# A streaming softmax: the exit of the engines with one barrier around the clearing of the semaphores instead of two

## The chip, the cores and the metric

One of the eight cores of a Trainium2 chip. The metric is the device time of one execution in microseconds; a profile of one execution comes with it. Most executions of this kernel agree within 0.3%. "Span" is the stretch from the first to the last profiled instruction; a store "lands" when its last semaphore update is in the trace.

## The reference

```python
x = np.random.randn(16, 1024, 512).astype(np.float32)
x_max = np.max(x, axis=-1, keepdims=True)
exp_x = np.exp(x - x_max)
return (exp_x / np.sum(exp_x, axis=-1, keepdims=True)).astype(np.float32)
```

A softmax over rows of 512 numbers: 33.55 MB in, 33.55 MB out.

## The kernel before

SyncE issues the loads, VectorE takes the row maxima and scales, ScalarE takes the exponentials and issues the stores. GpSimd and PE compute nothing in the body. The launch wraps the body in a context whose end adds an exit to every engine's program:

```python
with _tile.TileContext(nc) as tc:            # the launch line: L175 in the kernel before
    tile_softmax_online_kernel(tc, *args)
# ... cut: in the body, the last group's scaling ends with the last store
            nc.scalar.dma_start(
                out=dst[k][:, since:b, :], in_=place[k][:, since:b, :]
            )
```

This is the exit as it stands in the built program, engine by engine. "Gather" counts arrivals, "release" counts permissions to leave; `>=` and `== 0` are waits. A drain lets its engine's earlier work end first: VectorE's first one starts at 141.54 us and ends at 144.73, just after the last multiply.

```
SP    five semaphore waits and a drain: all loads, all stores, ScalarE, VectorE
ACT, PE, DVE, SP   drain, release == 0, gather += 1   (first arrival)
                   wait release >= 1, -= 1     (first leave)
                   drain, release == 0, gather += 1   (second arrival)
                   wait release >= 1, -= 1     (second leave)
POOL  drain
      wait gather >= 4, -= 4                   (first gather)
      release += 4                             (first release)
      drain
      clear the range of semaphores 99 to 108  (those of the body)
      drain
      wait gather >= 4, -= 4                   (second gather)
      release += 4                             (second release)
```

After it the runtime's own code runs; the profile does not show its instructions, but the trace has semaphore updates that come after the last profiled instruction, and I put these down to it.

Of the kernel before, what the change touches and what calls it, by code (L numbers as in the profile page):

```python
# [1 line left out]

# [4 lines left out]

F32 = mybir.dt.float32
EXP = mybir.ActivationFunctionType.Exp
AX = mybir.AxisListType.X  # L10


CHUNKS = [
    (3, 0), (5, 3), (8, 8), (16, 16), (16, 32), (16, 48), (16, 64), (16, 80), (16, 0), (16, 16),
]
SBUF_ROWS = 96

EARLY = 8
AFTER_STORE = {2: [8], 3: [9]}

GROUP = 8

FINISH_BEFORE = (1, 2, 3)

STORE_ROWS = {3: 8, 4: 8, 5: 8}

ON_ACT = ()

AT_HEAD = {mybir.EngineType.SP: 3}



def loads_at_the_head(nc):

    main, body = nc.main_func.blocks[0], nc.main_func.blocks[1]
    for engine, count in AT_HEAD.items():
        loads = [
            i
            for i in body.instructions
            if i.engine == engine and type(i).__name__ == "InstDMACopy"  # L40
        ][:count]
        barrier = next(
            n
            for n, i in enumerate(main.instructions)
            if i.engine == engine and type(i).__name__ == "InstDrain"
        )
        for load in loads:
            body.instructions.remove(load)
        main.instructions[barrier:barrier] = loads


@with_exitstack
def kernel(
    ctx: ExitStack,
    tc: tile.TileContext,
    x: bass.AP,
    out: bass.AP,
):
    nc = tc.nc
    nc.at_finalize(loads_at_the_head)  # L60
    P = nc.NUM_PARTITIONS

    x_flat = x.flatten_outer_dims()
    out_flat = out.flatten_outer_dims()
    n, d = x_flat.shape
    assert n == P * sum(R for R, _ in CHUNKS)


    src, dst, at = [], [], 0
    for R, _ in CHUNKS:  # L70
        for flat, views in ((x_flat, src), (out_flat, dst)):
            part = flat[at : at + P * R, :]
            views.append(part.rearrange("(p r) d -> p r d", r=R))
        at += P * R

    data = ctx.enter_context(tc.tile_pool(name="data", bufs=1))
    stats = ctx.enter_context(tc.tile_pool(name="stats", bufs=4))
    held = data.tile([P, SBUF_ROWS, d], F32, name="held")
    place = [held[:, s : s + R, :] for R, s in CHUNKS]


    groups = []
    for k, (R, _) in enumerate(CHUNKS):
        m = -(-R // GROUP)
        cuts = [R * i // m for i in range(m + 1)]
        since = 0
        for a, b in zip(cuts, cuts[1:]):
            ends = b == R or b - since >= STORE_ROWS.get(k, R)
            groups.append((k, a, b, since if ends else None))
            since = b if ends else since  # L90
    shift = [None] * len(groups)
    sums = [None] * len(groups)

    def load(k):
        queue = nc.scalar if k in ON_ACT else nc.sync
        queue.dma_start(out=place[k], in_=src[k])

    def rowmax(g):
        k, a, b, _ = groups[g]
        shift[g] = stats.tile([P, b - a], F32, name="shift", tag="shift")  # L100
        nc.vector.reduce_max(  # L101
            out=shift[g], in_=place[k][:, a:b, :], axis=AX, negate=True
        )

    def exps(g):
        k, a, b, _ = groups[g]
        sums[g] = stats.tile([P, b - a], F32, name="sums", tag="sums")
        for r in range(a, b):
            nc.scalar.activation(  # L109
                out=place[k][:, r, :],  # L110
                in_=place[k][:, r, :],
                func=EXP,
                bias=shift[g][:, r - a : r - a + 1],
                scale=1.0,
                accum_out=sums[g][:, r - a : r - a + 1],
            )

    def scale(g):
        k, a, b, since = groups[g]
        recip = stats.tile([P, b - a], F32, name="recip", tag="recip")  # L120
        nc.vector.reciprocal(out=recip, in_=sums[g])  # L121
        for r in range(a, b):
            nc.vector.tensor_scalar_mul(  # L123
                out=place[k][:, r, :],
                in0=place[k][:, r, :],
                scalar1=recip[:, r - a : r - a + 1],
            )
        if since is not None:
            nc.scalar.dma_start(
                out=dst[k][:, since:b, :], in_=place[k][:, since:b, :]  # L130
            )
        if b == CHUNKS[k][0]:
            for later in AFTER_STORE.get(k, ()):
                load(later)

    with tc.manual_schedule():
        for k in range(EARLY):
            load(k)
        waiting = None
        for g, (k, a, _, _) in enumerate(groups):  # L140
            if waiting is not None and a == 0 and k in FINISH_BEFORE:
                scale(waiting)
                waiting = None
            rowmax(g)
            exps(g)
            if waiting is not None:
                scale(waiting)
            waiting = g
        scale(waiting)


# [1 line left out]
_INS = ['x']  # L153
_OUTS = [((16, 1024, 512), 'float32')]


# [23 lines left out]
```

## Time and profile before

| | before |
|---|---|
| median time, 6 runs | 161.59 us (161.46 to 161.76) |
| span of the profiled instructions | 159.678 us |
| last store landed | 158.803 us |
| from that landing to the end of the span | 875 ns |
| from the end of the span to the runtime's last semaphore update | 1,901 ns |

The last two rows are what the argument is about: the exit, in the fourth, is half a percent of the time. Its instructions are semaphore instructions and drains, which the profile does not count as busy, so the engine shares, the slices and the chain of waits are blind to it. One finds it only by asking for the instructions of the launch line in the last two microseconds and by looking at where each starts. The prediction shows those lines.

### The profile page before, as it was taken

Reading aid. Unit: us, or ns where it says so; the run is one execution under the profiler, and the core shown is the slowest. Engines: PE = TensorE matmul, PEld = TensorE weight load, DVE = VectorE, ACT = ScalarE, POOL = GpSimd, SP = SyncE. Lnnn points to the kernel's source line nnn. Section 1 sums busy time; section 2 is a strip of 40 time slices with the busy share of each in tenths; the row PEclk is TensorE's granted clock in tenths of the full one; section 3 lists DMA queues with packets and bytes.
Section 4 is the critical chain, followed back from the end, with each engine's and each line's share of the span. In section 5 each row is a group of like instructions: output and inputs, shape, how many; then the busy total and the mean of one; then the engine's idle time right before and its main releaser. Section 6 shows DMA issues by size and latency. Waiting matters only on the chain.

```text
span 159.7 us, 521 instructions
## 1 busy us (share of the span) xinstructions
DVE 123.9 (78%) x162; ACT 93.3 (58%) x257; POOL 0.2 (0%) x4
## 2 busy tenths in 40 slices
DVE  0481870799699999999999999999999999762000
ACT  0718029208994959595867777686859594930000
POOL 0000000000000000000000000000000000000000
DMA  7999999899999999999999999999999999999993
GB/s 274 436 464 424 389 425 464 375 404 466 410 445 443 456 415 412 439 415 480 419 415 427 410 501 410 412 435 402 447 439 476 402 419 484 402 419 460 427 410 164
DMA packets 3315, 67.13 MB, mean 420 GB/s; under 512 B 368, under 2 KB 368, under 8 KB 624
## 3 DMA queue, kind: packets, MB, share of 16 engines
q1 hardware_dynamic: 1440, 33.56, 49.5%
q10 hardware_dynamic: 1872, 33.56, 48.9%
q14 instruction: 3, 0.02, 0.0%
HBM read 33.55 MB, written 33.55 MB: 420 GB/s over the span
## 4 chain that ended last, share of the span: by engine, by line
DVE 71%; ACT 14%; issue 3%; DMA 3%; DVEq 0%; ACTq 0%
DVE shift L101 38%; DVE held L123 30%; ACT held L109 14%; DMA held<-in_x_dram 3%; DVE recip L121 2%; DVEq L175 0%; ACTq L109 0%
## 5 line engine op out<-in xcount | busy, mean ns | idle before, releaser
L109 ACT ACTIVATE held<-held,shift 128x512 f32<-128x512 f32 x128 | 90.5, 708 | 43.4 <-DVE shift L101 33.3
L101 DVE TENSOR_REDUCE shift<-held 128x8 f32<-128x4096 f32 (+2 forms) x17 | 70.7, 4163 | 4.4 <-DMA held<-in_x_dram 4.4
L123 DVE TENSOR_SCALAR held<-held,recip 128x512 f32<-128x512 f32 x128 | 52.2, 482 | 0.6
L109 ACT ACTIVATION_READ_ACCUMULATOR held<-held,shift 128x1 f32 x128 | 23.9, 186 | 0.0
L121 DVE RECIPROCAL recip<-sums 128x8 f32<-128x8 f32 (+2 forms) x17 | 3.3, 195 | 15.8 <-ACT held L109 15.8
L109 ACT ACT_TABLE_LOAD x1 | 1.3, 1283 | 4.4 <-DMA held<-in_x_dram 4.4
L164 POOL MEMSET const-bfloat16-1.0<- 128x1 bf16 x1 | 0.1, 102 | 0.0
L164 POOL MEMSET const-uint8-127<- 128x1 uint8 x1 | 0.1, 102 | 0.0
L164 POOL MEMSET const-float32-1.0<- 128x1 f32 x1 | 0.1, 99 | 0.0
L164 POOL MEMSET const-float32-0.0<- 128x1 f32 x1 | 0.1, 98 | 0.2 <-issue 0.2
## 6 DMA issues: line engine op xcount, KB each, us to landing
held<-in_x_dram SPq DMA_DIRECT2D x7, 4096.0 KB, 41.8
out_dram<-held ACTq DMA_DIRECT2D x4, 4096.0 KB, 21.0
out_dram<-held ACTq DMA_DIRECT2D x7, 2048.0 KB, 35.4
held<-in_x_dram SPq DMA_DIRECT2D x1, 2048.0 KB, 11.4
held<-in_x_dram SPq DMA_DIRECT2D x1, 1280.0 KB, 7.0
out_dram<-held ACTq DMA_DIRECT2D x1, 1280.0 KB, 20.0
held<-in_x_dram SPq DMA_DIRECT2D x1, 768.0 KB, 4.4
out_dram<-held ACTq DMA_DIRECT2D x1, 768.0 KB, 15.8
```

Source lines behind the costliest of these rows:

```text
L101: nc.vector.reduce_max(out=shift[g], in_=place[k][:, a:b, :], axis=AX, negate=True)
L109: nc.scalar.activation(out=place[k][:, r, :], in_=place[k][:, r, :], func=EXP, bias=shift[g][:, r - a : r - a + 1], scale=1.0, accum_out=s ...
L121: nc.vector.reciprocal(out=recip, in_=sums[g])
L123: nc.vector.tensor_scalar_mul(out=place[k][:, r, :], in0=place[k][:, r, :], scalar1=recip[:, r - a : r - a + 1],)
L164: nc = _bacc.Bacc("TRN2", target_bir_lowering=False, num_devices=1)
```

## The change

The intent is to take one of the two barriers off the end of the kernel: the clear needs all engines to have arrived before it, and nobody to leave before it is done, and one gather ahead of it and one release behind it give both. A hook edits the exit block once the program's instructions are laid down (cut to the lines that matter):

```diff
+def one_barrier_on_exit(nc):
+    end = nc.main_func.blocks[2].instructions
+    def of(engine, kind):
+        return [i for i in end if i.engine == engine and type(i).__name__ == kind]
+    for engine in (... Activation, PE, DVE, SP ...):          # cut
+        arrivals = [i for i in of(engine, "InstDrain") if i.has_update()]
+        leaves = of(engine, "InstEventSemaphore")
+        assert len(arrivals) == len(leaves) == 2
+        end.remove(leaves[0])
+        end.remove(arrivals[1])
+    gather, release, gather_2, release_2 = of(mybir.EngineType.Pool, "InstEventSemaphore")
+    end.remove(release)
+    end.remove(gather_2)
...
     nc.at_finalize(loads_at_the_head)
+    nc.at_finalize(one_barrier_on_exit)
```

GpSimd keeps gather, drain, clear, drain, release. Nothing else in the program moves.

More of the change, by code (lines that the diff above doesn't have):

```diff
@@ L49, in loads_at_the_head @@
         main.instructions[barrier:barrier] = loads
+def one_barrier_on_exit(nc):
+    end = nc.main_func.blocks[2].instructions
+    def of(engine, kind):
+        return [i for i in end if i.engine == engine and type(i).__name__ == kind]
+    for engine in (
+        mybir.EngineType.Activation,
+        mybir.EngineType.PE,
+        mybir.EngineType.DVE,
+        mybir.EngineType.SP,
+    ):
+        arrivals = [i for i in of(engine, "InstDrain") if i.has_update()]
[6 more added lines that the diff above has]
+    end.remove(gather_2)
 @with_exitstack
```

## The prediction

> **What bounds the kernel now.** I read the page first, then the stretches of the last microseconds, then the launch line's own instructions there, then what SyncE waits for. The page's lines on busy time, the forty slices and the chain that ended last:
>
> ```profile
> DVE 123.9 (78%) x162; ACT 93.3 (58%) x257; POOL 0.2 (0%) x4
> ...
> DMA  7999999899999999999999999999999999999993
> ...
> HBM read 33.55 MB, written 33.55 MB: 420 GB/s over the span
> ...
> DVE 71%; ACT 14%; issue 3%; DMA 3%; DVEq 0%; ACTq 0%
> ```
>
> The sixteen DMA engines are at nine tenths or more in nearly every slice, VectorE at 78%, ScalarE at 58%. So this is a kernel that streams 67 MB and is held by its transfers. The chain by line is dominated by VectorE, but it ends with the last multiply at 144.7 us: it follows compute instructions, and none runs later. From there to 159.7 us the last store drains, and after it comes what this change edits. The stretches of the end (columns: stretch and its length, then busy us of VectorE, ScalarE, GpSimd, then the clock, the DMA share and GB/s):
>
> ```profile
> 150.00:155.00 5.00, 0.00 (x0) 0.00 (x0) 0.00 (x0) 1.00 1.06 459
> 155.00:156.00 1.00, 0.00 (x0) 0.00 (x0) 0.00 (x0) 1.00 0.68 295
> 156.00:157.00 1.00, 0.00 (x0) 0.00 (x0) 0.00 (x0) 1.00 1.14 492
> 157.00:158.00 1.00, 0.00 (x0) 0.00 (x0) 0.00 (x0) 1.00 0.16 66
> 158.00:159.00 1.00, 0.00 (x0) 0.00 (x0) 0.00 (x0) 1.00 0.00 0
> 159.00:160.00 1.00, 0.00 (x0) 0.00 (x0) 0.00 (x0) 1.00 0.00 0
> ```
>
> Data moves until about 158 us, and the last 1.7 us moves nothing. The last store was issued at 144.71 us and its semaphore is complete at 158.80 us. The waits of SyncE between 157 and 160 us (waiter, what it waited for, us in total, times, longest):
>
> ```profile
> SPq L175 <- DMA out_dram<-held: 9.6, 1, 9.6
> SPq L175 <- PEq L175: 0.6, 2, 0.4
> ```
>
> SyncE stood 9.6 us on the stores, so it is the last engine to arrive at the exit. The second line is the two releases it then waited for; the profile names PE there, but both come from GpSimd. The exit itself, as the launch line's instructions from 158 us on (engine, operation, count: ns shortest/median/longest, first and last start):
>
> ```profile
> L175 SPq EVENT_SEMAPHORE  x4: 17/22/28, 158.8 to 159.6; - x4
> L175 POOLq EVENT_SEMAPHORE  x4: 17/17/17, 159.0 to 159.6; - x4
> L175 SPq DRAIN  x3: 7/7/7, 158.9 to 159.2; - x3
> L175 ACTq EVENT_SEMAPHORE  x2: 17/17/17, 159.2 to 159.6; - x2
> L175 DVEq EVENT_SEMAPHORE  x2: 21/21/21, 159.2 to 159.6; - x2
> L175 PEldq EVENT_SEMAPHORE  x2: 51/51/51, 159.2 to 159.6; - x2
> L175 POOLq DRAIN  x2: 34/52/70, 159.2 to 159.4; - x2
> ...
> L175 POOLq EVENT_SEMAPHORE_RANGE_CLEAR  x1: 93/93/93, 159.3 to 159.3; - x1
> ```
>
> All of the two barriers and the clearing is here, between 159.0 us and the end of the span at 159.678 us. GpSimd's starts, to the nanosecond from the trace's records, are: gather 159.037, release 159.115, drain 159.196, clear 159.295, drain 159.417, second gather 159.495, second release 159.574. The others pass the first release at 159.157 to 159.169 and the second at 159.615 to 159.627; PE's takes 51 ns and ends the span.
>
> **What the Trainium skill says.** "Perfetto Trace Analysis", section "Sequencer-only Instruction (DRAIN, etc)", says that only the execution of such an instruction is in the record, while waiting for a semaphore and spreading its update are not. The trace agrees: GpSimd's semaphore instructions record 17 ns each, yet the next instruction starts 78 to 81 ns after such a one starts. So I cost each instruction by the distance between starts, not by its duration. "VectorE: DVE Perf Modes", section "The DRAIN you can't avoid", puts boilerplate drains at about 12 ns on all engines. Here they take 7 to 19 ns on the four arriving engines, but 34 and 70 ns on GpSimd, the one that matters; the measurement decides. "Runtime: NRT & Kernel Launch", section "The ~15µs preamble/postamble breakdown", lists a barrier and semaphore reset that the runtime adds after the kernel. The time before is 161.66 us and the span 159.68 us, so about 2.0 us lies outside the profiled instructions; the change touches none of it.
>
> **The change part by part.** The body is untouched: the build shows the same sequence of loads, stores and compute on every engine. The end block falls from 30 instructions to 20.
>
> *Removed from ACT, PE, DVE and SP*: the first leave and the second arrival, two instructions each. These ran at 159.157 to 159.34 us, beside GpSimd's drain and clear. The second arrivals start at 159.249 to 159.319 us, and the latest is recorded as an update at 159.341 us, 154 ns before GpSimd's second gather starts at 159.495. They held nobody up, so removing them is worth 0 by itself.
>
> *Removed from GpSimd*: the first release and the second gather. GpSimd was on the path throughout: no other engine could leave before its second release, and it waited for nobody after 159.04 us. The first release costs the distance from its start to the drain's: 159.196 - 159.115 = 81 ns. The second gather costs the distance to the second release: 159.574 - 159.495 = 79 ns. Sum 160 ns.
>
> *Kept on the path*: gather, drain, clear, drain, one release, the leave. From the same SyncE arrival: gather at 159.037, drain 78 later at 159.115, clear 99 later at 159.214, drain 122 later at 159.336, release 78 later at 159.414, then 104 ns from that release to the end of PE's leave (159.574 to 159.678), ending at 159.518 us. That is 159.678 - 159.518 = 0.160 us less.
>
> *Added*: nothing. Nor does the clear come too early: it runs after all four have arrived, and SyncE arrives only after it has seen the last store's semaphore. The cleared numbers (98 to 108) do not include the barrier's own two (96 and 97), so a count in flight is not lost.
>
> Time: 161.66 - 0.16 = 161.50 us, or 0.1% less.
>
> **The rivals.** *A whole barrier is saved.* From GpSimd's drain at 159.196 us to the end is 482 ns, and a barrier without a clear might seem to cost most of that: 161.2 us. Against it: 99 + 122 ns of that stretch is the drain and the clear, which stay, and the exit after the release stays too. Even this would be 0.3%.
>
> *The clear moves into the wait and is hidden.* Were the clear done while SyncE still waits for stores, the path would lose another 0.2 us (161.3 us). Against it: the clear still stands after the gather in GpSimd's order, so it starts after the last arrival.
>
> *A new wait takes the removed one's place.* The four engines now sit at one release from their arrival on, and the runtime's own barrier follows. If that barrier, or the sequencers' fetching after a longer wait, absorbed the gain, the time would stay 161.66. For it: the profile shows nothing of the runtime's code but its length. Against it: before, too, all engines leave within 12 ns of one another on one release and enter that code together, so the shape should only shift. Instruction fetches were at 44.6, 61.0 and 101.5 us, none near the exit.
>
> *The gain drowns.* Three runs before spread over 0.24 us, more than the 0.16 expected, because the body's transfers vary. This rival concerns what is seen, not what happens, and I think it likely with three runs.
>
> **Range and chances.** Mechanism: 0.16 us, with 0.08 (one of the two instructions absorbed) to 0.3 as its outer bounds, so 161.36 to 161.58. The spread of the runs before, about 0.12 us either side, and a shift between sessions widen this to 161.20 to 161.78. For faster by 2% the kernel would have to lose 3.2 us; the entire stretch from SyncE's arrival to the end is 0.67 us. Within 2% is nearly certain; I leave 1% for each side, for a disturbed session.
>
> **What would show it.** GpSimd should have two semaphore instructions at the exit in place of four, still two drains and one clear, and the other engines one semaphore instruction and one arriving drain each. From SyncE's arrival to the end of the span should be near 0.51 us in place of 0.67. From GpSimd's gather to its drain should be near 78 ns and from its second drain to the release near 78 ns; if either is near 160, the removed instruction's time was a wait and not a step. If the exit shrinks but the difference between the time and the span grows, the runtime's barrier took the gain. The store's landing at 158.8 us should move only by run-to-run noise; if it moves by more than 0.3 us, the comparison of single profiles says nothing of the exit. The prediction would be wrong if the body changed, which the build denies, or if engines left the release apart.

## The result, and the profile after

The changed kernel took 161.41 us, median of 6 runs (161.38 to 161.66), against 161.59 us before (161.46 to 161.76). A ratio here is the mean time of one kernel's fast runs over that of the other's in the same rounds, so not quite the ratio of the medians. It is 0.9991, with a 95% interval from 0.9979 to 1.0004: the same within 2%, and by these runs alone not even surely below 1.

The page of the changed kernel, the lines that answer to those of before (busy time, slices, bytes, chain by engine), with the line of the span:

```profile
span 159.6 us, 511 instructions
...
DVE 123.9 (78%) x162; ACT 93.3 (58%) x257; POOL 0.2 (0%) x4
...
DMA  7999999899999999999899999999999999999993
...
HBM read 33.55 MB, written 33.55 MB: 421 GB/s over the span
...
DVE 71%; ACT 14%; issue 3%; DMA 3%; DVEq 0%; ACTq 0%
```

There are ten instructions fewer, and otherwise it is the same page: the body is untouched, and on this scale the exit is invisible. What SyncE waits for between 157 and 160 us, after the change:

```profile
SPq L199 <- DMA out_dram<-held: 9.6, 1, 9.6
SPq L199 <- PEq L199: 0.5, 1, 0.5
```

There is one wait for a release now, where before there were two (0.6 us in all). The launch line is L199 in the changed kernel; its instructions from 158 us on (engine, operation, count: ns shortest/median/longest, first and last start in us):

```profile
L199 SPq EVENT_SEMAPHORE  x3: 17/27/28, 158.9 to 159.5; - x3
L199 SPq DRAIN  x2: 7/7/7, 159.0 to 159.1; - x2
L199 POOLq EVENT_SEMAPHORE  x2: 17/17/17, 159.1 to 159.5; - x2
L199 POOLq DRAIN  x2: 34/52/70, 159.2 to 159.4; - x2
L199 POOLq EVENT_SEMAPHORE_RANGE_CLEAR  x1: 93/93/93, 159.3 to 159.3; - x1
...
L199 PEldq EVENT_SEMAPHORE  x1: 51/51/51, 159.5 to 159.5; - x1
```

GpSimd has two semaphore instructions where it had four, and PE one where it had two. The starts of GpSimd's instructions from the trace's records, in ns after its first gather, and the end of the span on the same scale:

```
          gather  release  drain  clear  drain  gather  release   end of span
before         0       78    159    258    380     458      537           641
changed        0        -     81    180    302       -      365           469
```

The exit is 172 ns shorter: 78 ns between the gather and the first drain (159 to 81) and 94 ns between the second drain and the release (157 to 63). The stretch ahead of the gather is 234 ns from the last landing in both kernels, so the landing to the end went from 875 to 703 ns. Yet the profiled execution's time fell by only 0.05 us, 161.46 to 161.41. Part of that is the body: its last store landed 80 ns later in this execution (158.883 us). The rest is outside the span: the time less the span is 1.782 us before and 1.824 us after.

So three questions were left. Is the saving the two GpSimd steps, or a hand-over between engines that went with them? Does the time follow the exit at all? And where do the 42 ns outside the span come from?

### The profile page after: what moved, and what is told of

It is laid out like the page before. It is cut to its first block, busy times and chain, and to the rows that moved or that the text cites. A ratio compares the mean times of both kernels' runs of the same rounds, so it can differ in the third digit from the quotient of the medians.

```text
span 159.6 us, 511 instructions
## 1 busy us (share of the span) xinstructions
DVE 123.9 (78%) x162; ACT 93.3 (58%) x257; POOL 0.2 (0%) x4
## 2 busy tenths in 40 slices
DMA packets 3315, 67.13 MB, mean 421 GB/s; under 512 B 368, under 2 KB 368, under 8 KB 624
## 4 chain that ended last, share of the span: by engine, by line
DVE 71%; ACT 14%; issue 3%; DMA 3%; DVEq 0%; ACTq 0%
DVE shift L125 39%; DVE held L147 30%; ACT held L133 14%; DMA held<-in_x_dram 3%; DVE recip L145 2%; DVEq L199 0%; ACTq L133 0%
```

## The experiments

Theory: each GpSimd instruction between the last arrival and the release is a step of about 80 ns on the path, whether it waits for anyone or not, and the change saves two steps. Rivals: the saving is the round trip to the other engines; or what follows the exit absorbs what the exit saves. Lengths below are of one execution's trace, "landing" is the last store's. All kernels gave correct results. `like(i, ...)` makes a copy of an exit instruction with other waits or updates, `sync(i, ...)` puts such a copy in its place.

### The changed kernel again, five rounds

> The changed kernel again, with more rounds. My theory (two steps of GpSimd left the path, and the runtime's part after the exit is unchanged): from the last store's landing to the end of the span 0.70 us where the kernel before has 0.875, and a time 0.16 to 0.18 us below the kernel before, ratio 0.9989 to 0.9990. Rival (what follows the exit absorbs the gain): ratio 1.000 with an exit of 0.70 us all the same.

Landing to end: 703 ns. Median 161.44 us (161.40 to 161.48) against 161.66 us, ratio 0.9985, interval 0.9972 to 0.9997: just below 1. The means differ by 0.24 us (161.68 and 161.44), more than the exit gives; the nine runs before spread from 161.55 to 161.93 us. So the sign is confirmed, if barely, but the time alone cannot tell 0.13 us from 0.17 us here; the larger edits below test that better. The time less the span averages 1.84 us in these five runs and 1.78 us in the nine before (each rounded to 0.1 us in the span), and this kernel's own trace has 1.837 us, so the 42 ns of the two profiles was no accident.

### One half: only the first release gone

```diff
-    end.remove(leaves[0]); end.remove(arrivals[1])
-    end.remove(release); end.remove(gather_2)
+    end.remove(leaves[0])
+    end.remove(release)
+    # each engine arrives twice in a row; the first gather waits for all eight
+    sync(gather, wait=[changed(w, wait_value=8) for w in gather.sync_info.on_wait])
```

> One half of the change: GpSimd's first release and the four first leaves are gone, the second barrier's arrivals and gather stay, and the first gather waits for both arrivals of each engine (8) so that the clear stays safe. My theory: from GpSimd's first gather to the end of the span 641 - 81 = 560 ns, since one GpSimd step is gone; the second arrival of SyncE adds some 58 ns ahead of the gather, so the landing to the end is about 0.85 us. Rival (the saving is in the second gather, which waits for arrivals): 641 ns from the first gather to the end, the gather being on the path as before.

Gather to end: 563 ns; the first drain starts 81 ns after the gather, and the second gather stays 78 ns behind the second drain. SyncE's second arrival cost 77 ns where 58 were expected (311 ns from the landing to the gather), so the landing to the end is 874 ns and not 850: this half gained a GpSimd step and gave a SyncE step back. Theory right, rival (641 ns) out. It shows why halves of such an edit need care: an instruction that was hidden before lay on the path here.

### The other half: the second gather gone, a step in the release's place

```diff
     end.remove(leaves[0]); end.remove(arrivals[1])       # as in the change
-    end.remove(release)
+    # the release becomes an addition to a body semaphore that nobody waits for any more
+    sync(release, update=[changed(u, id=99, update_value=1) for u in release.sync_info.on_update])
     end.remove(gather_2)
```

> The other half: second arrivals, second gather and first leaves are gone, but in the place of the first release GpSimd keeps one semaphore instruction that adds 1 to a semaphore that nobody waits for by then (it is cleared next). My theory (what counts is the number of GpSimd steps, about 80 ns each, whether or not anyone is released): 469 + 80 = 549 ns from the gather to the end of the span, against 641 before and 469 after the change. Rival (the cost is the hand-over to the four engines and their return): 469 ns, as with the whole change.

Gather to end: 547 ns, 78 more than the changed kernel and 94 less than before. So the two halves, 78 for the first release (above) and 94 for the second gather, add up to the 172 of the whole. An instruction that releases nobody costs as much as the first release did. The hand-over to the other engines was worth nothing: the 78 ns are GpSimd's step.

### The step by itself, ten times

```diff
+    # on top of the last edit: ten of the idle additions in a row, between the gather and the drain
+    end[at:at] = [like(step) for _ in range(9)]
```

> The disputed cost by itself, ten times: the changed kernel with ten such idle semaphore instructions on GpSimd between the gather and the drain. My theory: 10 x 80 = 0.80 us more than the changed kernel from the gather to the end (1.27 us), and the time too rises by 0.80 us over the changed kernel, 0.63 us over the kernel before (ratio 1.0039), since what follows the exit absorbs nothing. Rival one (the runtime's part absorbs exit time): the span grows but the time stays. Rival two (an instruction that releases nobody costs only its recorded 17 ns): 0.17 us more.

The launch line's instructions in this kernel, from 159.1 us on, the GpSimd lines:

```profile
L233 POOLq EVENT_SEMAPHORE  x12: 17/17/17, 159.4 to 160.5; - x12
...
L233 POOLq DRAIN  x2: 34/52/70, 160.2 to 160.4; - x2
L233 POOLq EVENT_SEMAPHORE_RANGE_CLEAR  x1: 93/93/93, 160.3 to 160.3; - x1
```

Twelve instructions of 17 ns fill more than a microsecond: the records of their starts lie 78 or 79 ns apart, and the gather to the end is 1,253 ns, 784 more than in the changed kernel. The time rose with it: the mean is 162.27 us, 0.83 us above the changed kernel in the same session (161.44). Ratio to the kernel before 1.0033 (1.0017 to 1.0048). So what follows the exit absorbs nothing of this size, and a recorded duration of 17 ns is not the cost.

### Ten more whole barriers

```diff
+    for n in range(10):        # after the exit: every engine arrives and leaves, GpSimd gathers and releases
+        for engine in four:
+            more += [like(arrival), like(leave)]
+        more += [like(gather), like(release)]
```

> The changed kernel with ten more whole barriers (arrive, gather, release, leave) after its exit. My theory: a bare barrier costs its round trip, worked out from the trace of the kernel before: gather to release 78 ns, release to PE's leave 54, leave to PE's next arrival 150, arrival to gather 33, together 315 ns; so 3.15 us more span and time than the changed kernel (time ratio to the kernel before 1.018). It is more than the 0.17 us that the change saved, because the removed barrier's round trip lay beside the drain and the clear. Rival (a barrier costs what the change saved): 1.7 us more. Rival two (the 482 ns from the drain to the end are a barrier's price): 4.8 us more.

The launch line's instructions from 158.9 us on:

```profile
L235 POOLq EVENT_SEMAPHORE  x22: 17/17/17, 159.1 to 162.8; - x22
...
L235 PEldq EVENT_SEMAPHORE  x11: 51/51/51, 159.5 to 162.8; - x11
...
L235 PEldq DRAIN  x10: 7/8/8, 159.7 to 162.7; - x10
```

Ten barriers took 3,315 ns, 331 each on average: gather to release 78, release to the next gather 249 in the common case, so 327. PE arrives last each time; once, where its arrival came some 80 ns after VectorE's and not 40, the barrier took 366. The exit is 3,142 ns longer than before the change, and the mean time 3.11 us longer (164.70 and 161.59 us; ratio 1.0192, 1.0178 to 1.0206, an interval that holds the 2% mark). Both rivals are out: a bare barrier costs neither the 172 ns that the change saved nor 482. The theory's sum of 315 ns was 5% short: PE's arrival to the gather takes 44 ns in the first of them, and the 33 of the sum were SyncE's. The change saved half a barrier because the other half, the second arrivals, had run beside the drain and the clear.

### Without the drains around the clear

```diff
+    for drain in of(mybir.EngineType.Pool, "InstDrain")[1:]:
+        end.remove(drain)
```

> The changed kernel without GpSimd's two drains around the clear. My theory (each remaining GpSimd instruction is a step on the path): gather to clear about 80 ns, clear to release 93 + 30 = 123 ns, release to the end 104 ns, so 307 ns from the gather to the end against 469; about 0.16 us saved. Rival (the drains cover a time in which the clear or its spreading must finish anyway): the release moves little, and more than 400 ns remain.

Gather to end: 308 ns. The clear starts 81 ns after the gather and the release 122 ns after the clear, as if the drains had never stood between. Another 161 ns gone, and the rival (the drains cover a time that must pass anyway) is out. That they may be dropped safely is less than shown: the result was right, and GpSimd has nothing in flight at this point; its last compute instructions are the four memsets at the start.

### GpSimd waits for the last store itself

In the changed kernel SyncE sees the last landing, then passes one more wait, a drain and its arrival, and only then does GpSimd start: 234 ns after the landing.

```diff
+    store = [w for w in waits if w.id == 107]      # the last store's semaphore
+    rest = [w for w in waits if w.id != 107]
+    sync(last, wait=rest)                          # SyncE no longer waits for it
+    sync(gather, wait=list(gather.sync_info.on_wait) + store)
```

> The changed kernel, with the wait for the last store moved from SyncE to GpSimd's gather: SyncE arrives early, and GpSimd goes on straight from the landing. My theory: SyncE's three steps and its arrival (234 ns from the landing to the gather's start) fall to about 20 ns; the landing to the end is 0.02 + 0.47 = 0.49 us against 0.70, and the time 0.21 us below the changed kernel, 0.38 below the kernel before (ratio 0.9976). Rival (a wait for two semaphores on GpSimd is slower, or wakes late): no gain, 0.65 us or more.

Landing to end: 482 ns (0.49 us expected). The mean time is 161.22 us against 161.59, ratio 0.9977 (0.9961 to 0.9992).

### Both shortenings together

> Both shortenings together on the changed kernel: GpSimd waits for the last store itself, and the two drains around the clear are gone. My theory: 0.02 + 0.31 = 0.33 us from the landing to the end, against 0.875 before: 0.55 us off the time, ratio 0.9966, clear of 1. Rival (what follows the exit has its own floor): the exit shrinks to 0.33 us but the time by less than 0.4 us.

The launch line's instructions from 149 us on:

```profile
L236 SPq DRAIN  x2: 7/7/7, 149.4 to 149.4; - x2
L236 POOLq EVENT_SEMAPHORE  x2: 17/4740/9463, 149.5 to 159.1; - x2
L236 POOLq EVENT_SEMAPHORE_RANGE_CLEAR  x1: 93/93/93, 159.0 to 159.0; - x1
...
L236 PEldq EVENT_SEMAPHORE  x1: 51/51/51, 159.2 to 159.2; - x1
```

SyncE has arrived at 149.4 us; GpSimd's gather stands until the landing (its record of 9,463 ns includes the wait), then one clear, one release, and everyone leaves. Landing to end: 320 ns, 555 less than before. Median 161.05 us (161.00 to 161.07) against 161.58 us, ratio 0.9965 (0.9953 to 0.9978), clear of 1. The mean time fell by 0.55 us. It is faster than the kernel before by a third of a percent; the changed kernel was not run in the same rounds (161.44 us in the rounds above).

### The 42 ns outside the span

Every kernel above in which PE has one or two exit instructions fewer than before (all but the one with ten more barriers) had 1.94 to 1.95 us from the end of its span to the runtime's last semaphore update. The kernel before had 1.901 and the kernel with ten more barriers 1.906. I asked whether that holds, and whether it follows from the number of instructions in an engine's program.

> The kernel before once more, for a second trace. From the end of the span to the runtime's last semaphore update its first trace has 1.901 us, and seven traces of one-barrier exits have 1.941 to 1.947. My theory now (the stretch after the exit really is some 40 ns longer with the short exit, so of 172 ns gained in the span about 130 reach the time): 1.90 us again, landing to end 875 ns again. Rival (one odd trace): 1.94 us.

> The changed kernel with two idle drains at the head of SyncE's exit, which run while it waits for the stores, so that SyncE has as many instructions in the exit as before the change. Theory (the runtime's part after the exit depends on where SyncE's instructions stand in its stream): the exit stays 703 ns and the stretch after the span falls to 1.90 us, the time minus the span to 1.78. Rival (it depends on another engine, or on the time between SyncE's instructions): 1.94 us and 1.82 to 1.84.

> The same with two idle drains ahead of every engine's arrival, GpSimd too; all run beside the wait for the stores, and every engine has as many instructions as before the change. Theory (the place of instructions in a stream, on whichever engine): exit 703 ns, stretch after the span 1.90 us. Rival (it is not the place of instructions, but what the engines did shortly before the runtime's code): 1.94 us.

> The shortest exit so far (GpSimd waits for the last store, no drains around the clear) with two idle drains on PE alone, ahead of its arrival, which run beside the wait for the stores. Padding all engines brought the stretch after the span back from 1.94 to 1.90 us, padding SyncE alone did not, and kernels in which GpSimd has eight instructions more or one less still have 1.94; so it is PE, ScalarE or VectorE. Theory (it is PE): exit 320 ns, stretch after the span 1.90 us, time some 0.59 us below the kernel before (ratio 0.9963). Rival (ScalarE or VectorE): 320 ns, 1.945 us, ratio 0.9965 as without the padding.

The edit of the last three puts two drains that wait for nothing at the head of an engine's exit, where they run well before the last landing (PE's at 1.8 and 1.9 us, since PE has no work in the body):

```diff
+    end[at:at] = [like(idle, [], [], engine) for _ in range(2)]   # SP / all five / PE alone
```

| kernel | landing to end, ns | end of span to the runtime's last update, ns | time less span, us |
|---|---|---|---|
| before | 875 | 1,901 | 1.782 |
| before, second trace | 876 | 1,905 | 1.782 |
| changed | 703 | 1,941 | 1.824 |
| changed, SyncE padded | 704 | 1,940 | 1.828 |
| changed, all engines padded | 704 | 1,901 | 1.790 |
| both shortenings | 320 | 1,945 | 1.838 |
| both shortenings, PE padded | 320 | 1,902 | 1.790 |

The 40 ns are real; two idle instructions on PE take them away again, and padding SyncE does not. PE's two ran some 157 us before the end, so what counts is not what PE does shortly before the runtime's code. The trace's updates say where the 40 ns lie: there are five blocks of updates, each over its own range of semaphores, and the one over 7 to 53 starts and ends last, beginning 972 ns after the end of the span before, and 1,015 ns after it in the changed kernel; the four other blocks begin within 10 ns of where they did. That PE makes these updates fits the padding, but no record names their engine. Why one or two instructions fewer on PE go with a later end is open; the place of its program in memory is a guess. (The last update lies later after the span, 1.90 us, than the time less the span, 1.78; where the timed stretch begins and ends, no record says.)

The padded version's median is 161.00 us (160.99 to 161.27, ratio 0.9968, interval 0.9955 to 0.9982), not told apart from 161.05 us by these times: the mean of its five runs is raised by one of 161.27 us.

## Why the prediction was right or wrong

**The time, 161.50 us in a range from 161.20 to 161.78, and "within 2%":** right; 161.41 us was measured. But the range holds 161.66, no change at all, so the time alone says nothing for the mechanism; the traces do. That the first times would hardly show the gain was right too.

**What bounds the kernel:** not put to the test here. The body is the same line for line, its shares did not move, and the length that changed by design lies behind the last landing.

**The arrivals and leaves of the four engines are worth nothing by themselves:** right inside the span, where the two GpSimd steps, 78 and 94 ns, account for the whole 172. The one half shows GpSimd's step saved with the second arrivals in place, and the other half shows the step kept with no one released. Behind the span, PE's two removed instructions were not free (see below).

**Two GpSimd steps, 81 + 79 = 160 ns:** right in mechanism, 12 ns short. The first release was worth 78 (predicted 81). The second gather was worth 94 (predicted 79). The step that failed is "release 78 later", the distance from the second drain to the release, which I took from the drain and the gather of before. It measured 63 ns. In all three traces in which a semaphore instruction with a wait follows that drain it starts 78 ns after it, even where its wait was long satisfied, and in the eight in which one without a wait follows, 63 or 64 ns after it. The distance from gather to drain, put at 78 as well, measured 81; together -15 and +3 make the 12 ns. From SyncE's arrival to the end of the span it was 501 ns (0.51 us predicted, 674 ns before).

**Nothing given back outside the span:** this failed. "The change touches none of it" was wrong by some 40 ns, a quarter of the gain, and the padding of PE shows that it goes with the two instructions removed from PE. ("About 2.0 us" for that stretch was the median of three runs less the span of another execution; within one execution it is 1.782.) The prediction had named this sign, a difference between time and span that grows, but put it down to the runtime's barrier. That is not where it lies: the first nine updates of semaphore 2 after the span, which I take for that barrier, come at the same distance, within 2 ns, in both kernels, and the last nine all come 39 to 41 ns later, after the block over 7 to 53.

**The rivals.** *A whole barrier is saved* is out, and its price is known: 331 ns for a bare one, not 482. *The clear hidden in the wait* was not tried and did not happen: the clear starts after the gather in every trace. *A new wait*: a quarter of the gain was given back, as above, but later than the runtime's first updates; whether fetching has a part in it is open. *The gain drowns* held for the first six runs; in five rounds the interval just cleared 1.

**A slip:** the prediction says that numbers 98 to 108 are cleared. The instruction clears 99 to 108. The argument from it (the barrier's own two are not among them) stands.

## What to carry to other kernels

Find who is on the path of a barrier before counting its instructions: here one engine's steps of about 80 ns were the whole gain, and eight removed instructions on the other four engines gained nothing (two of them, PE's, went with some 40 ns more behind the exit). An exit of 0.9 us could be cut to 0.3 us, most of it not by merging barriers but by letting the engine that clears wait for the last store itself and by dropping drains on an idle engine, for which each kernel needs its own check. For a kernel of 160 us that is a third of a percent; it is worth the care only where kernels are short or everything larger is done.

## What the Trainium skill lacked or had wrong

- "VectorE: DVE Perf Modes", section "The DRAIN you can't avoid", gives the drains that the runtime adds before and after a kernel as about 12 ns on all engines. The drains of this exit belong to the program, so these runs don't contradict that; no page has a duration for them. The ones that had nothing to wait for on their engine took 7 to 8 ns on SyncE, ScalarE and PE, 10 to 19 on VectorE, and 34 and 70 on GpSimd; and taking GpSimd's two away saved 161 ns, more than they record.
- "Perfetto Trace Analysis", section "Sequencer-only Instruction (DRAIN, etc)", says that waits and updates are outside the record but gives no size for the step. On GpSimd a semaphore instruction of 17 ns costs 78 ns, measured ten in a row. It also has the record start only when all semaphores are satisfied. With one wait that fits (17 ns for GpSimd's gather); but GpSimd's gather with two waits recorded 9,463 ns: it starts when the arrivals are in, and the wait for the landing is inside.
- "Runtime: NRT & Kernel Launch", section "The ~15µs preamble/postamble breakdown", lists about 1.5, 1.5 and 2 us for what follows a kernel. Here the runtime's last semaphore update came 1.90 to 1.95 us after the end of the span; that the two name the same stretch is not shown. It moved by some 40 ns with two instructions of PE's program; no page has that.
- No page has the price of a barrier in which one engine gathers the other four and releases them: 331 ns here, when nothing else runs beside it. (The pages have a figure for the runtime's own barrier, which passes from engine to engine.)
